# RWKV-7 + MLA + PEER block: the inverse's diagonal blocks through a DRAM tile of their own, four gates' weights in another pool

## The chip, the cores and the metric

One core of a Trainium2 chip runs the whole kernel in one launch. The metric is the device time of one execution in microseconds (us); less is better. The time of a kernel is the median of several executions.

## What is computed

One transformer-like block on T = 512 tokens of width 1024, in float32. The normed input is multiplied by one large matrix `w_in`; its columns are cut into three parts: 15 chunks of 128 columns for an RWKV-7 time mix, 4 for a latent attention (MLA), and 16 for gates. Both mixes run on the same input, each is projected back, multiplied by a sigmoid gate and added; a PEER layer (16,384 experts, top 16 of 8 heads) and a small gated projection follow. Cut to what matters here:

```python
def rwkv7_scan(r, a_vec, b_vec, v, k, decay):
    def step(state, inp):
        r_t, a_t, b_t, v_t, k_t, w_t = inp
        sa = jnp.einsum('bdhvk,bdhk->bdhv', state, a_t)
        state = (state * w_t[..., None, :] + sa[..., :, None] * b_t[..., None, :]
                 + v_t[..., :, None] * k_t[..., None, :])
        return state, jnp.einsum('bdhvk,bdhk->bdhv', state, r_t)
...
def hybrid_rwkv7_mla_peer_block(...):
    u = rmsnorm(x, g_mix) @ w_in
    y_rw = rwkv7_time_mix(u[..., :RW_COLS], ...)
    y_mla = mla_mix(u[..., RW_COLS:RW_COLS + MLA_COLS], ...)
    g = sigmoid(u[..., RW_COLS + MLA_COLS:])
...
```

The scan runs in two directions (d = 0, 1) over 8 heads of width 64. It is not computed token by token: the kernel cuts the 512 tokens into 8 chunks of 64, builds for each chunk, head and direction a 64x64 triangular matrix from products of the vectors, and needs the inverse of that triangle. It inverts the two 32x32 diagonal blocks of each (128 of these pairs: 2 directions, 8 heads, 8 chunks) and gets the rest by matmuls.

## The kernel before

The work around the change has three stages. Everything is written with a tile framework: a tile belongs to a pool with a number of buffers, the framework puts in the semaphores, and a scheduler that simulates the program sets the order of the instructions of each engine. Every engine then executes its own list in that order. A pool that is allocated where a released pool stood waits for the last use of the released pool's tiles.

**Preparation (`prep`, L353 on, driven together with `others` and the first six gates from L641 on).** For each pair of heads c = 0 to 3 and direction d it makes the scan's vectors and calls three helpers. `gram` (L453) forms the products of the vectors on TensorE (PE, L464), masks them on VectorE (DVE) into a tile `gm` (L466, 3 buffers) in two halves of four chunks, and stores each half by two DMAs that POOL issues (L470) into the DRAM tile `pk_d`, the packed operands of the scan. Then SyncE (SP) reads the 32x32 diagonal blocks back from `pk_d` into the tile `U` (L478): 4 DMAs per call, of 8 partitions x 32 rows x 32 numbers, so 32 in all. Last DVE multiplies `bk` by the decay (L480). `bkt_` (L482) transposes `bk` on PE (L488), copies it on ScalarE (ACT, L489) and POOL stores it (L491). `v_t` does the same for `v` (L496 to L505) and makes `bonus` (L508 to L511). After the last of them the pool of this stage, `P`, is released, and the pools of the next stage (`YM`, `M`, `GW`) are allocated.

**The inverse, the gates and the start of attention (L944 on).** `inverse` (L555) does the 128 inversions at once, one pair of blocks per partition: 31 steps, k from 31 down to 1, each a product `xtmp` (L567) and a sum into `X` (L570) for each of the two blocks b = 0, 1, so 124 DVE instructions in sequence. `X` is stored (L574, L575) for the scan's chain. Beside it, gates 6 to 15 are computed. A gate (`gates`, L634) is one chunk of `w_in`: SP loads the raw weights of 512 KB (`wload`, L123; 3 raw buffers `wraw`), ACT rounds them into `whi` (L132), DVE makes the rest `wlo` (L133), PE does 24 matmuls of 128x512 (`mm3`, L137 to L143: for each of the 8 slices one with `whi` and `xh`, one with `whi` and `xl`, one with `wlo` and `xh`), ACT takes the sigmoid (L637), SP stores it (L638). `whi` and `wlo` come from a pool that the caller names or, without a name, from the pool `s.W` (2 buffers, shared with the weights of the attention). The loop at L947 gives gates 6 to 9 no pool; the one at L952 gives gates 10 to 15 the pool `GW`, which has 2 buffers and lies where `P` lay.

```python
inverse()
rest = attn()
for _ in gates(NG, NG + GK, GT):
    pass
...
for _ in gates(NG + GK, 16, GT, GW):
    pass
GW.release()
CH = pool(name="ch", bufs=2)
drive(chain(), rest, ...)
```

NG is 6, GK is 4; GT is the PSUM tag `mm`, whose two buffers the gates share with the first matmuls of the attention: 12 for `vt` (L831), split by ACT and DVE (L147, L148), then the first projections (`proj_k`, `proj_q`; their splits are `kl`, `ql` on L148 and `rt` on L854 to L856) and scores (L874).

**The chain (`chain`, L652).** Its pool `CH` lies where `GW` lay, and its operands `pk` are loaded into the space of `xh` and `xl`, which the gates read. So its first work, two memsets on POOL (L657) and the load of `pk` (L667), waits for the last gate's last matmul. Its steps are then interleaved with the attention.

In the changed kernel the lines from 274 on stand one further down, and those behind the new store in `gram` five further: L638 there is L643, L567 is L572, L464 is L465, L488 is L493. The new store is L473.

Of the kernel before, what the change touches and what calls it, by code (L numbers as in the profile page):

```python
# [20 lines left out]
F32 = mybir.dt.float32  # L21
# [91 lines left out]
def phase1(nc, tc, A, dbg):  # L113

    s = K()
# [65 lines left out]
    def mm_tile(shape=(128, 512), tag="mm"):  # L181
        return (ppc if tag in "cu" else pp).tile(list(shape), F32, name=tag, tag=tag, bufs=1 if tag == "u" else None)
# [76 lines left out]
    def uchunk(oc, tag="mm", pl=None, raw=None):  # L259
        hi, lo = raw or wload(A["w_in"][oc], pl)  # L260
        ps = mm_tile(tag=tag)
        mm3(ps, hi, lo, *(XR if raw else (xh, xl)), [(k, k) for k in range(8)])
        return ps
# [6 lines left out]
    pk_d = gdram.tile([16, 128, 2048], F32, name="pk_d")  # L270
    v_d = gdram.tile([128, 8, 8, 64], F32, name="v_d")
    x_d = gdram.tile([128, 2, 32, 32], F32, name="x_d")
    xt_d = gdram.tile([128, 32, 32], F32, name="xt_d")

    s.WX = pool(name="w0", bufs=1, side="right")
    MU = pool(name="mu", bufs=2)
# [5 lines left out]
    U = R.tile([128, 2, 32, 32], F32, name="U", tag="Oa")  # L282
# [52 lines left out]
    def prep():  # L335
# [117 lines left out]
        def gram(c, d):  # L453

            AR = B["ar", c, d]
            BKf = B["bk", c, d].rearrange("p c a t -> p c (a t)")
            for half in range(2):
                gm = P.tile([128, 4, 2, 2, 64], F32, name="gm", bufs=3)
                for q in range(2):
                    sl = slice(q * 64, q * 64 + 64)  # L460
                    ps = mm_tile((128, 4, 128), tag="c")
                    for i in range(4):
                        cc = half * 4 + i
                        nc.tensor.matmul(ps[:, i], BKf[sl, cc], AR[sl, cc].rearrange("p a t -> p (a t)"),  # L464
                                         start=True, stop=True)  # L465
                    nc.vector.tensor_mul(gm[:, :, q], ps.rearrange("p i (a t) -> p i a t", a=2),  # L466
                                         mask[:, None].to_broadcast([128, 4, 2, 64]))
                gf = gm.rearrange("p c q a t -> p c (q a t)")
                for e, r0, o in ((1, d * 64, c * 256), (0, 64 - d * 64, d * 1024 + c * 256)):
                    (nc.gpsimd, nc.sync)[GQ if e else 0].dma_start(  # L470
                        pk_d[half * 8 + e:half * 8 + 8:2, r0:r0 + 64, o:o + 256].rearrange("k s t -> s k t"),
                        gf[r0:r0 + 64])

            for q in range(2):
                for b in range(2):
                    r0, p0 = d * 64 + b * 32, d * 64 + (2 * c + q) * 8
                    o = (2 * c + q) * 128 + b * 32
                    nc.sync.dma_start(U[p0:p0 + 8, b], pk_d[1::2, r0:r0 + 32, o:o + 32])  # L478

            nc.vector.tensor_mul(BKf, BKf, WC[:, d, c, :, None].to_broadcast([128, 8, 128]))  # L480

# [38 lines left out]
        for c in range(4):  # L520
            u_k(c)
            w_a(c, 0)
            u_r(c)
            k_norm(c)
            abkr(c, 0)
            yield UNS
            w_a(c, 1)
            if c:
                gram(c - 1, 1)
                u_v(c)  # L530
                bkt_(c - 1, 1)
                v_t(c - 1)
            else:
                u_v(c)
            abkr(c, 1)
            if c == 2:
                shifted(14, lg)
                nc.scalar.activation(lg, lg, AF.Sigmoid)
            yield UNS
            if c < 3:  # L540
                gram(c, 0)
                yield 100
                bkt_(c, 0)
        gram(3, 0)
        gram(3, 1)
        yield UNS
# [86 lines left out]
    def gates(i0, i1, tag="u", pl=None):  # L633
        for i in range(i0, i1):  # L634
            ps = uchunk(19 + i, tag, pl)
            gt = MU.tile([128, T], F32, name="gt")
            nc.scalar.activation(gt, ps, AF.Sigmoid)  # L637
            nc.sync.dma_start(gates_d[i], gt)  # L638
            yield UNS
# [9 lines left out]
    GW = pool(name="gw", bufs=2)  # L649
# [294 lines left out]
    inverse()  # L944
    Oa = R.tile([128, 4, T], F32, name="Oa")
    rest = attn()
    for _ in gates(NG, NG + GK, GT):  # L947
        pass
    if PRE:
        while next(rest) >= 0:  # L950
# [93 lines left out]
GT = "mm"  # L1044
# [6 lines left out]
GK = 4  # L1051
NG = 6
# [495 lines left out]
```

## Time and profile before

| what | value |
|---|---|
| median of 3 executions | 1909.32 us (1908.85 to 1920.4) |
| the profiled execution: its own time | 1914.83 us |
| its span, first to last instruction | 1912.7 us |
| outside the span (difference) | 2.1 us |
| mean granted TensorE clock | 0.982 |

The profile is of one execution. Times in its rows count from the span's start. PE is TensorE's matmuls, PEld its weight loads, DVE VectorE, ACT ScalarE, POOL GpSimd, SP SyncE (which here only issues DMAs; SPq is its queue of instructions). A row of a timeline gives start, length, engine, line, operation, output and inputs, how many instructions it joins, and in brackets how long the engine had been idle and for what. Matmuls overlap in their records: one that takes 0.39 us in its row starts 0.23 us after the one before. The stages named above lie at about 187 to 263 us (the end of preparation), 263 to 329 us (inverse and gates) and from 329 us (chain).

### The profile page before, as it was taken

To read this page: it belongs to the slowest core of one execution; us is meant where nothing else is said; L and a number is where in the kernel's file an instruction comes from. 1 tells how busy PE (TensorE), PEld (TensorE's weight loads), DVE (VectorE), ACT (ScalarE), POOL (GpSimd) and SP (SyncE) were. 2 spreads that over 40 slices of the span, in tenths; PEclk is the share of its full clock that TensorE was granted. 3 is DMA by queue.
4 is the path that set the end of the run, shared out by engine and by line. 5 is a ranking of instruction groups with operands and counts; after the bars stand their busy time and mean duration, and the time that the engine had idled before them with its cause. 6 is when DMAs were issued, how large, how long until landed. Compare 5 with 4: busy or idle time off the path is not lost.

```text
span 1912.7 us, 29780 instructions
## 1 busy us (share of the span) xinstructions
PE 1821.6 (95%) x10969; PEld 1569.8 (82%) x10969; DVE 1540.8 (81%) x3103; ACT 827.2 (43%) x1224; POOL 468.4 (24%) x449
## 2 busy tenths in 40 slices
PE   7999869999999998999999999999999999999997
PEld 6777647777677888999999989888888888888775
DVE  6865778889855889999898965878788788778777
ACT  4755533666334333444444433333333333333354
POOL 1012331220101000332233021334344354344100
PEclk9999989999999999999999999999999999999999
DMA  4355664763434333889999899899999999999862
GB/s 166 90 151 174 165 179 144 226 204 105 149 105 143 100 100 100 260 289 347 339 342 327 307 354 350 315 338 340 338 335 343 322 352 340 340 327 335 280 214 99
DMA packets 196721, 470.19 MB, mean 246 GB/s; under 512 B 33312, under 2 KB 100896, under 8 KB 192736
## 3 DMA queue, kind: packets, MB, share of 16 engines
q1 hardware_dynamic: 146688, 273.23, 43.4%
q0 software_dynamic: 49744, 194.80, 28.7%
q8 instruction: 86, 1.41, 0.3%
q14 instruction: 59, 0.48, 0.1%
q10 hardware_dynamic: 144, 0.26, 0.0%
HBM read 397.97 MB, written 70.25 MB: 245 GB/s over the span
## 4 chain that ended last, share of the span: by engine, by line
PE 69%; DVE 13%; DMA 10%; issue 5%; ACT 3%; POOL 0%; SPq 0%; DVEq 0%; POOLq 0%; ACTq 0%
PE po L1498 20%; PE pa L1150 7%; PE pa L1148 7%; PE pa L1149 7%; DMA row<-in_v,e 6%; PE mm L141 3%; PE mm L142 3%; PE mm L143 3%; DVE wlo L133 2%; PE po L1377 2%; PE q L141 2%; PE q L142 2%; PE q L143 2%; DVE acc L1103 1%; DMA gt<-gates_d 1%
## 5 line engine op out<-in xcount | busy, mean ns | idle before, releaser
L132 ACT ACTIVATE whi<-wraw 128x1024 fp32r<-128x1024 f32 x352 | 370.4, 1058 | 429.7 <-PE pa L1149 157.4
L133 DVE TENSOR_TENSOR wlo<-wraw,whi 128x1024 fp32r<-128x1024 f32 x352 | 428.3, 1221 | 89.6 <-ACT whi L132 82.9
L1150 PE MATMUL pa<-hh,wlo 128*128 128x384 f32 x1024 | 348.9, 341 | 4.3 <-DVE wlo L133 4.3
L1148 PE MATMUL pa<-hh,whi 128*128 128x384 f32 x1024 | 348.9, 341 | 3.5 <-ACT gs L1156 2.5
L1149 PE MATMUL pa<-hl,whi 128*128 128x384 f32 x1024 | 348.3, 340 | 0.0
L1085 POOL DMA_INDIRECT row<-in_u,e x128 | 165.6, 1293 | 423.9 <-DVE row L1093 326.9
L1498 PE MATMUL po<-wlo,wh 128*128 128x512 f32 x768 | 239.1, 392 | 4.3 <-DVE wlo L133 4.3
L1085 POOL DMA_INDIRECT row<-in_v,e x128 | 178.5, 1395 | 248.6 <-DVE acc L1103 234.2
L1498 PE MATMUL po<-whi,wl 128*128 128x512 f32 x768 | 238.4, 392 | 0.0
L1498 PE MATMUL po<-whi,wh 128*128 128x512 f32 x768 | 211.0, 390 | 4.5 <-issue 3.4
L1103 DVE SCALAR_TENSOR_TENSOR acc<-row,pre,acc 128x1024 f32<-128x1024 f32 x127 | 162.7, 1281 | 54.8 <-DMA row<-in_v,e 54.2
L1148 PEld LDWEIGHTS pa<-hh,whi 128*128 128x128 f32 x1024 | 193.2, 189 | 8.2 <-ACT gs L1156 3.2
L1150 PEld LDWEIGHTS pa<-hh,wlo 128*128 128x128 f32 x1024 | 193.0, 189 | 6.6 <-DVE wlo L133 4.6
L1149 PEld LDWEIGHTS pa<-hl,whi 128*128 128x128 f32 x1024 | 193.0, 188 | 3.8
L1498 PEld LDWEIGHTS po<-wlo,wh 128*128 128x128 f32 x768 | 144.6, 189 | 32.4 <-DVE wlo L133 5.1
L1498 PEld LDWEIGHTS po<-whi,wl 128*128 128x128 f32 x768 | 145.3, 189 | 30.9
L1093 DVE SCALAR_TENSOR_TENSOR row<-row,h2t 128x1024 f32<-128x1024 f32 x128 | 155.4, 1220 | 17.5 <-DMA row<-in_u,e 17.4
L1498 PEld LDWEIGHTS po<-whi,wh 128*128 128x128 f32 x768 | 143.0, 188 | 29.4 <-issue 3.6
L147 ACT ACTIVATE wh<-gl 128x384 fp32r<-128x384 f32 x72 | 37.9, 526 | 214.3 <-PE po L1498 214.2
L147 ACT ACTIVATE wh<-ga 128x384 fp32r<-128x384 f32 x48 | 25.2, 524 | 128.2 <-PE po L1498 83.2
L141 PE MATMUL mm<-xh,whi 128*128 128x512 f32 x184 | 74.5, 405 | 4.9 <-ACT gt L637 3.3
L1297 ACT ACTIVATE st<-g 128x512 f32<-128x512 f32 x96 | 50.9, 600 | 54.3 <-PE g L1296 54.3
(465 smaller groups left out, 3178.7 us busy)
## 6 DMA issues: line engine op xcount, KB each, us to landing
wraw<-in_uT SPq DMA_DIRECT2D x128, 512.0 KB
wraw<-in_v SPq DMA_DIRECT2D x128, 512.0 KB
gd<-st POOLq DMA_DIRECT2D x12, 2048.0 KB, 8.2
g<-gd SPq DMA_DIRECT2D x32, 768.0 KB
wraw<-in_w_in SPq DMA_DIRECT2D x35, 512.0 KB
pk<-pk_d SPq DMA_DIRECT2D x16, 1024.0 KB
ga_d<-gs SPq DMA_DIRECT2D x72, 192.0 KB
gl<-ga_d SPq DMA_DIRECT2D x72, 192.0 KB
```

Of the source, the lines that this page charges most:

```text
L132: nc.scalar.activation(hi, raw, AF.Copy)
L133: (nc.gpsimd if s.nw <= NWP else nc.vector).tensor_sub(lo, raw, hi.bitcast(F32))
L141: nc.tensor.matmul(out, hi[:, kw], xh[:, kx], start=(i == 0), stop=False)
L142: nc.tensor.matmul(out, hi[:, kw], xl[:, kx], start=False, stop=False)
L143: nc.tensor.matmul(out, lo[:, kw], xh[:, kx], start=False, stop=(i == n - 1))
L1085: nc.gpsimd.indirect_dma_start(out=r, out_offset=None, in_=table, in_offset=bass.IndirectOffsetOnAxis(ap=e3[:, hk:hk + 1], axis=0))
L1093: nc.vector.scalar_tensor_tensor(r, r, 1.0, h2t, op0=OP.mult, op1=OP.mult, accum_out=pre[:, u:u + 1])
L1103: nc.vector.scalar_tensor_tensor(acc, r, pre[:, u:u + 1], acc, op0=OP.mult, op1=OP.add)
L1148: nc.tensor.matmul(pa, hi[:, k], hh[:, k, 0:NDT], start=(k == 0), stop=False)
L1149: nc.tensor.matmul(pa, hi[:, k], hl[:, k, 0:NDT], start=False, stop=False)
L1150: nc.tensor.matmul(pa, lo[:, k], hh[:, k, 0:NDT], start=False, stop=(k == 7))
L1498: nc.tensor.matmul(po[tb][:, half], w[:, ts], v[:, hs], start=(m == 0 and w is wh and v is vh), stop=(m == 127 and w is wl))
```

## The change

There are two edits. First, `gram` stores the diagonal blocks a second time: for each half, block b and head of the pair q, SP issues one DMA from `gm` into a new DRAM tile `u_d` (32 rows, 4 chunks, 32 numbers), so 8 per call and 64 in all. The reads of `U` come from `u_d` and no more from `pk_d`; there are 2 per call, 16 in all, and each moves 16 rows of 1024 numbers in one piece. Second, gates 6 to 9 are given the pool `GW`.

```diff
+    u_d = gdram.tile([8, 2, 2, 8, 32, 32], F32, name="u_d")
...
+                for b in range(2):
+                    r0 = d * 64 + b * 32
+                    for q in range(2):
+                        nc.sync.dma_start(u_d[d * 4 + c, b, q, half * 4:half * 4 + 4].rearrange("k s t -> s k t"),
+                                          gm[r0:r0 + 32, :, q, 0, b * 32:b * 32 + 32])
                 gf = gm.rearrange("p c q a t -> p c (q a t)")
...
-            for q in range(2):
-                for b in range(2):
-                    r0, p0 = d * 64 + b * 32, d * 64 + (2 * c + q) * 8
-                    o = (2 * c + q) * 128 + b * 32
-                    nc.sync.dma_start(U[p0:p0 + 8, b], pk_d[1::2, r0:r0 + 32, o:o + 32])
+            p0 = d * 64 + c * 16
+            for b in range(2):
+                nc.sync.dma_start(U[p0:p0 + 16, b], u_d[d * 4 + c, b].rearrange("q k s t -> (q k) s t"))
...
-    for _ in gates(NG, NG + GK, GT):
+    for _ in gates(NG, NG + GK, GT, GW):
         pass
```

The scheduler then makes other lists. On PE, before, two gates stand among the last small matmuls of preparation (the first rows of gate 6, behind the products L464 of the pair c = 2; ident is the identity of a transpose):

```order
L488 MATMUL c<-ident,bk 128x128 x8
L503 MATMUL c<-ident,vRS 128x128 x8
L510 MATMUL c<-sht,same 128x512
L464 MATMUL c<-ar,bk 128x128 x16
L141 MATMUL mm<-xh,whi 128x512
L142 MATMUL mm<-xl,whi 128x512
L143 MATMUL mm<-xh,wlo 128x512
```

The same place on PE after the change, up to the first matmul of gate 6:

```order
L227 MATMUL c<-ident,spr 128x128 x4
L415 MATMUL c<-lw,w_242 128x512
L419 MATMUL c<-la,a_244 128x512
L465 MATMUL c<-ar,bk 128x128 x16
L493 MATMUL c<-ident,bk 128x128 x8
L508 MATMUL c<-ident,vRS 128x128 x8
L515 MATMUL c<-sht,same 128x512
L465 MATMUL c<-ar,bk 128x128 x32
L493 MATMUL c<-ident,bk 128x128 x16
L508 MATMUL c<-ident,vRS 128x128 x8
L515 MATMUL c<-sht,same 128x512
L141 MATMUL mm<-xh,whi 128x512
```

The 48 matmuls of gates 6 and 7 have left preparation: all ten gates now stand behind its last matmul, in the order 6, 7, 8, 9, the 12 matmuls of `vt`, the first projections, and 10 to 15. The four `whi` on ACT and the four `wlo` on DVE that belong to gates 6 to 9 have left preparation with them.

On DVE, before, the first `wlo` beside the inverse (that of the attention's weights) stands here, at the steps of 135 and 156 numbers (X_2056 and X_2057 are the two blocks):

```order
L570 TENSOR_TENSOR X_2056<-X_2056,xtmp 128x27x5
L570 TENSOR_TENSOR X_2057<-X_2057,xtmp 128x27x5
L133 TENSOR_TENSOR wlo<-wraw,whi 128x1024
L567 TENSOR_TENSOR xtmp<-U,X_2056 128x156
L567 TENSOR_TENSOR xtmp<-U,X_2057 128x156
```

After the change the first `wlo` on DVE beside the inverse are those of gates 6 and 7:

```order
L572 TENSOR_TENSOR xtmp<-U,X_2105 128x192
L572 TENSOR_TENSOR xtmp<-U,X_2106 128x175
L133 TENSOR_TENSOR wlo<-wraw,whi 128x1024
L575 TENSOR_TENSOR X_2105<-X_2105,xtmp 128x24x8
L575 TENSOR_TENSOR X_2106<-X_2106,xtmp 128x25x7
L133 TENSOR_TENSOR wlo<-wraw,whi 128x1024
L148 TENSOR_TENSOR cql<-cqn,cqh 128x512
```

The `wlo` of gate 6 stands behind 28 instructions of the inverse and one for `bonus`; the two blocks now run one step apart. Further down DVE's list, before, the two `kl` splits, which free the PSUM buffer that gate 10 takes, stand among the growing steps:

```order
L567 TENSOR_TENSOR xtmp<-U,X_2056 128x252
L567 TENSOR_TENSOR xtmp<-U,X_2057 128x252
L148 TENSOR_TENSOR kl_2373<-mm,kh_2370 64x512
L570 TENSOR_TENSOR X_2056<-X_2056,xtmp 128x18x14
L570 TENSOR_TENSOR X_2057<-X_2057,xtmp 128x18x14
L567 TENSOR_TENSOR xtmp<-U,X_2056 128x255
L148 TENSOR_TENSOR kl_2374<-mm,kh_2371 64x512
```

After the change they stand here on DVE:

```order
L148 TENSOR_TENSOR kl_2422<-mm,kh_2419 64x512
L572 TENSOR_TENSOR xtmp<-U,X_2105 128x207
L572 TENSOR_TENSOR xtmp<-U,X_2106 128x220
L575 TENSOR_TENSOR X_2105<-X_2105,xtmp 128x9x23
L575 TENSOR_TENSOR X_2106<-X_2106,xtmp 128x10x22
L148 TENSOR_TENSOR kl_2423<-mm,kh_2420 64x512
```

The second `kl` has 90 of the inverse's 124 instructions ahead of it, and 8 `wlo`; before it had 57 and 4. SP's list at the end of preparation, after the change, is nine stores to `u_d`, a read of `U`, a store, a read, six stores, two reads; the raw weights of gates 6 to 8 are loaded before these, that of gate 9 behind them.

## Rows read from the trace of the kernel before

**Rows 1.** Stretches: length, busy (instructions) by engine, PEclk granted, DMA share, GB/s.
```profile
210.00:228.00 18.00, 16.58 (x75) 11.82 (x74) 10.01 (x18) 12.10 (x14) 3.40 (x5) 1.00 0.54 184
228.00:259.20 31.20, 21.04 (x144) 16.44 (x143) 23.05 (x35) 13.10 (x20) 16.43 (x23) 0.89 0.84 226
259.20:272.70 13.50, 13.42 (x49) 10.18 (x49) 9.20 (x21) 4.65 (x8) 5.56 (x6) 0.87 0.29 91
272.70:293.60 20.90, 8.75 (x20) 5.00 (x21) 20.18 (x51) 6.54 (x10) 0.00 (x0) 0.67 0.44 126
293.60:329.20 35.60, 35.58 (x153) 28.66 (x154) 29.01 (x84) 11.60 (x15) 0.00 (x0) 1.00 0.41 141
329.20:480.00 150.80, 137.80 (x2182) 111.91 (x2181) 134.06 (x291) 98.09 (x191) 28.02 (x51) 0.94 0.59 180
```

**Rows 2.** POOL's timeline: beside the inverse's start, and the chain's first work.
```profile
265.52 3.80 POOL L840 TENSOR_TENSOR kl<-krt,kh 32x512 fp32r<-32x512 f32 x3
329.68 1.06 POOL L657 MEMSET Xs<- 128x512 f32 x2 [60.37 <-PE mm L143]
```

**Rows 3.** PE's waits, 240 to 345 us: waiting line, releaser, us, times, longest.
```profile
PE mm L831 <- DVE wlo L133: 6.4, 1, 6.4
...
PE mm L831 <- DVE vt L148: 2.9, 1, 2.9
...
PE mm L141 <- DVE kl L148: 1.6, 1, 1.6
```

**Rows 4.** DVE's timeline: end of preparation, start of the inverse, `kl`, late step.
```profile
211.94 1.21 DVE L480 TENSOR_TENSOR bk<-bk,wc 128x1024 f32<-128x1024 f32 x1
...
227.00 1.22 DVE L133 TENSOR_TENSOR wlo<-wraw,whi 128x1024 fp32r<-128x1024 f32 x1
228.13 0.68 DVE L402 TENSOR_TENSOR kk<-kk,c 128x512 f32<-128x512 f32 x1
...
250.12 1.28 DVE L466 TENSOR_TENSOR gm<-c,mask 128x512 f32<-128x512 f32 x2
...
263.35 0.50 DVE L567 TENSOR_TENSOR xtmp<-U,X 128x31 f32<-128x31 f32 x2 [6.71 <-DMA U<-pk_d]
...
265.54 2.61 DVE L570 TENSOR_TENSOR X<-X,xtmp 128x60 f32<-128x60 f32 x2
...
292.79 0.69 DVE L148 TENSOR_TENSOR kl<-mm,kh 64x512 fp32r<-64x512 f32 x1
...
320.78 0.35 DVE L570 TENSOR_TENSOR X<-X,xtmp 128x60 f32<-128x60 f32 x2
```

**Rows 5.** ACT's timeline: first work in the space of preparation's pool.
```profile
263.42 1.68 ACT L147 ACTIVATE cqh<-cqn 128x512 fp32r<-128x512 f32 x3 [4.22 <-DMA pk_d<-bkt]
```

**Rows 6.** PE's timeline: gate 6 and the transposes behind it, the last gate matmul.
```profile
210.11 0.50 PE L141 MATMUL mm<-xh,whi 128*128 128x512 f32 x1
...
215.79 1.03 PE L488 MATMUL c<-ident,bk 128*128 128x128 f32 x8
...
329.17 0.40 PE L143 MATMUL mm<-xh,wlo 128*128 128x512 f32 x1
```

**Rows 7.** Issue of the reads of `U`: ns min/median/max, first and last start.
```profile
L478 SPq DMA_DIRECT2D U<-pk_d x32: 264/365/1242, 107.0 to 259.3; - x32
```

**Rows 8.** The stores L470 by POOL: from issue to landing.
```profile
DMA to landing us min/median/max: 3.1/4.1/6.0
```

**Rows 9.** The chain of waits, 200 to 420 us: start, length, what.
```profile
259.26 4.26 DMA U<-pk_d
```

**Rows 10.** DMA, 200 to 262 us: SP's queue: packets, MB, share of 16 engines.
```profile
q1 hardware_dynamic: 5487, 2.26, 14.2%
```

**Rows 11.** DVE by line, 263.3 to 321.5 us: busy us, mean ns, idle before.
```profile
L570 DVE TENSOR_TENSOR X<-X,xtmp 128x31 f32<-128x31 f32 (+15 forms) x62 | 21.3, 377 | 0.0
L567 DVE TENSOR_TENSOR xtmp<-U,X 128x31 f32<-128x31 f32 (+15 forms) x62 | 20.8, 367 | 6.9 <-DMA U<-pk_d 6.7
L133 DVE TENSOR_TENSOR wlo<-wraw,whi 128x1024 fp32r<-128x1024 f32 x8 | 9.8, 1219 | 0.5 <-ACT whi L132 0.4
```

## The prediction

> **What bounds the kernel now.** I read the stretches around the change first, then the first work of the stage that follows it, then PE's waits, and last the timelines of DVE, ACT and PE. A change here counts by what it does to the start of the chain: from 329.2 to 480 us PE is busy for 137.80 of 150.80 us and DVE for 134.06 [rows 1], so a stage that starts later has little slack to catch up with. What releases the chain is plain: its first memset on POOL had been waiting for 60.37 us and starts 0.1 us after the last gate matmul [rows 2, 6]. The inverse does not release it: its last steps run at 320.78 [rows 4], over 8 us earlier.
>
> So the question is when the tenth gate ends. The reader sees two very different stretches ahead of it. From 293.6 on PE is full (35.58 of 35.6 us) with 153 matmuls: six gates of 24 and 9 of scores, 0.2325 us each, 5.6 us for a gate. From 272.7 to 293.6 it is busy for only 8.75 of 20.9 us, at a granted clock of 0.67, while DVE is busy for 20.18 [rows 1]. The waits name DVE each time: 6.4 us for a `wlo`, 2.9 us for a `vt` split, 1.6 us for the `kl` split that frees gate 10's PSUM buffer [rows 3]. DVE is the bound of this stage, by its order: inverse and splits share one list. Gates 6 to 9 hardly feel it in the kernel before, because gates 6 and 7 are computed during preparation and the weights of 8 and 9 are split there.
>
> **The end of preparation.** The second edit takes two gates, four `whi` and four `wlo` out of it. Gate 6 holds PE from 210.11 to 215.79, and the transposes L488 come right behind; their input `bk` was ready at 211.94 + 1.21 = 213.15 [rows 4, 6], so they can start 2.6 us earlier. The `wlo` at 227.00 keeps `kk` until 228.13: another 1.1 us [rows 4]. Together 3.8 us. Bounds: 1.1 us if only the last of these lies on the path; 7.8 if the other gate's and splits' time does too (gate 7's 5.6 us and the 2.2 us of two more `wlo`). I take 3.8, the sum of the two that I can point at. Then the last `gm`, done at 250.12 + 1.28 = 251.40 [rows 4], comes at 247.6, and the last store of `bkt`, for which the first ACT work in the old pool's space waits until 263.42 [rows 5], lands at 259.6. That store matters more than it did: gates 6 and 7 now take `GW`, in that space, so no `whi` for them can be written before.
>
> **The short way to U.** Before, 263.35 - 251.40 = 11.95 us pass from the last `gm` to the first step of the inverse [rows 4]. After, they are four stores of 0.365 us to issue, 1.5 us [rows 7]; a landing; two reads to issue, 0.7 us; a landing. No row shows a store of 16 KB or a read of 16 rows of 4 KB. POOL's stores of 256 KB land after 3.1 to 6.0 us, 4.1 in the median [rows 8]; the old read took 4.26 in the chain [rows 9]. Two landings are thus 6.2 at the least and 12 at the most by these rows, the whole way 8.4 to 14.2. I take 9.0, near the low end, because both transfers move less than those timed. The inverse starts at 256.6, 6.8 us earlier. Bounds, with those of preparation: 252.0 and 264.5.
>
> Each piece of the new stores is 128 bytes, 64 times 128 pieces in all. SP's queue, whose pieces in this stretch were nearly all of that size, took 14.2% of 16 engines over 62 us, 141 us of engine time for 5487 packets, 26 ns each [rows 10]; 512 pieces of the last half call, spread over 16 engines, are 0.8 us. Inside the bounds. The Trainium skill (DMA: Bandwidth & Descriptors, Specifications) speaks against the edit: under 512 bytes a transfer falls short of line rate, since the engine reads and writes back. No row here prices a store of that size; were it to double the packet's 26 ns, the 0.8 us would be 1.6 and the forecast 0.8 us later. The same page (Anatomy of one DMA) gives about 2.0 us plus bytes over 436e3 for a DMA that POOL issues, by which both landings together would be an estimated 4.2 us, the inverse would start about 2.6 us earlier than in my sum and the forecast would be 1916; the 3.1 us that the fastest of 32 stores took here [rows 8] says no.
>
> **Gates beside the inverse.** This is where the gain goes. In DVE's new list the `wlo` of gate 6 has 28 steps of the inverse ahead of it and the second `kl` has 90, with 8 `wlo`; before they were 57 and 4. One step costs 0.34 us: the lines L567 and L570 have 42.1 us busy for 124 instructions [rows 11] (their records, 377 and 367 ns in the mean, overlap a little). A `wlo` costs 1.13, as the one at 227.00 does before `kk` [rows 4]. From the inverse's start to the end of the second `kl` there were 30.1 us [rows 4]; now 33 more steps, 11.2 us, 4 more `wlo`, 4.5 us, and the `bonus` instruction, 0.6 us: 46.4 us. Bounds: 42.6 if POOL's `kl`, 3.80 us from 265.52 on, no longer meets the inverse (the pair of 60 numbers took 2.61 us beside it, and 0.35 later on [rows 2, 4]), 49 if DVE waits for weights twice. I take 46.4, since POOL's `kl` follows the same store as before and still falls into the inverse.
>
> So `kl` is done at 256.6 + 46.4 = 303.0, and gate 10 starts there. Behind it stand the same six gates and 8 or 9 matmuls of scores, 35.6 us [rows 1]: the last gate ends at 338.6 instead of 329.17 + 0.4, 9 us later. PE by itself would be sooner: gate 6 cannot finish before its `wlo`, about 256.6 + 28 x 0.34 + 0.6 + 1.1 = 267.8; from there 92 matmuls of gates 6 to 9, 12 of `vt` and 9 of projections (26.3 us), 1.8 us for a clock that is low after the pause (13.5 us at 0.87 granted where gate 8 starts [rows 1]), and 35.6: 331.5, 1.9 us later than before. The later one decides; some 7 us of PE's pause in front of gate 10 stay.
>
> The sum: 9 us on the profiled 1914.83 us. Its span of 1912.7 and the 2.1 us around it are 5.5 us over the median of the executions shown, so on the median the forecast is 1909.3 + 9 = 1918 us. The inverse itself, with all 12 `wlo` in its list, ends about where it did, and nobody waits for that.
>
> **Rivals.** *The short way reaches the chain (faster).* Gates need no split in time, PE runs without pause from the first `whi`. It can start at 259.6 + 1.06, and ten gates, `vt`, projections and scores are 240 + 12 + 9 + 9 matmuls, 62.8 us, with 1.8 for the clock: 325.3, 4.3 us sooner, 1905 us. For it: preparation does become shorter, and PE's total work is unchanged. Against it: DVE must have the `wlo` of gate 6 by 261 and the second `kl` 35.6 us before the end. It decides if the inverse starts before about 247, where the last `gm` is only just made; or if DVE's list matters less than its records say.
>
> *No change to speak of.* PE's bound above holds instead of DVE's: +1.9 us, 1911 us. For it: PE idles 12 of 20.9 us before [rows 1], room for the moved gates. It needs DVE to lose the 3.8 us of POOL's `kl` and the inverse to start 3.3 us sooner than I say.
>
> *SP becomes the bound (slower still).* SP works strictly in order: each read of `U` waits for stores to land, and behind it wait the next stores, whose `gm` (3 buffers) cannot be written again until they land. In the last two calls a store, a read, a store and a read stand singly in the list. Two more waits of one landing, 4.1 us each [rows 8], delay the last `gm` and with it all that follows: +17 us, 1926 us. For it: the reads of `U` came last before the inverse already [rows 4]. Against it: with three buffers two halves are in flight.
>
> **How the numbers follow.** The forecast, +4 to +14 us, gets 0.5; no change, -2 to +4, 0.22; the faster rival, -2 to -8, 0.13; SP's, over +14, 0.15. A measurement of this kernel tells about 1% from no change, 19 us. Only the tails pass it: SP's rival with a third wait, 0.05 slower; a faster rival of four times its price, 0.03. Leaving one in ten on each side gives 1904 to 1930 us; the forecast's own range is 1913 to 1923.
>
> **What would show it.** Right: first step of the inverse at 255 to 259 us; preparation's last PE work about 4 us sooner; first gate matmul at about 260, then a pause of several us for `wlo`; PE idle again before gate 10 with DVE named; POOL's first memset of the chain at 335 to 341 us. Wrong: that memset before 329.7; or an inverse that starts no earlier, with SP's queue waiting for stores to `u_d`; or a full PE between 268 and 300 us, which would mean that DVE was not the bound.

## The result and the profile after

The changed kernel takes 1938.83 us (median of 4 executions, 1935.74 to 1939.6); the kernel before, beside it, 1909.87. The ratio of the times is 1.0129, 95% interval 1.0104 to 1.0154, which is 25 us slower; the two medians differ by 29. The forecast was 1918, the range ended at 1930. The sign and the place were right and the size was not.

The profiled execution has a span of 1937.4 us, 24.7 more than before. The first memset of the chain on POOL shows that 21.2 of them are there already (329.68 before [rows 2]):

```profile
350.88 1.07 POOL L662 MEMSET Xs<- 128x512 f32 x2 [76.96 <-PE mm L143]
```

The other 3.5 us are behind it. In the ten profiles below in which the whole computation is done, the span behind this memset is between 1576 and 1591 us (1583.0 before, 1586.5 after), with and without the stores, so these 3.5 us can't be told from nothing, and the runs below are compared by their moments up to the memset first.

DVE's timeline of the changed kernel shows the same moments as [rows 4], with the first `wlo` (that of gate 6):

```profile
225.00 0.69 DVE L403 TENSOR_TENSOR kk<-kk,c 128x512 f32<-128x512 f32 x1 [1.27 <-PE c L227]
...
243.70 2.63 DVE L467 TENSOR_TENSOR gm<-c,mask 128x512 f32<-128x512 f32 x4 [0.39 <-PE c L465]
...
253.57 1.29 DVE L467 TENSOR_TENSOR gm<-c,mask 128x512 f32<-128x512 f32 x2 [3.03 <-DMA u_d<-gm]
267.27 0.20 DVE L572 TENSOR_TENSOR xtmp<-U,X 128x31 f32<-128x31 f32 x1 [12.41 <-DMA u_d<-gm]
...
278.05 1.23 DVE L133 TENSOR_TENSOR wlo<-wraw,whi 128x1024 fp32r<-128x1024 f32 x1 [0.21 <-issue]
...
314.25 0.69 DVE L148 TENSOR_TENSOR kl<-mm,kh 64x512 fp32r<-64x512 f32 x1
```

`kk` is 3.1 us earlier than before. The four `gm` behind it are not; before they started at 243.37:

```profile
243.37 2.63 DVE L466 TENSOR_TENSOR gm<-c,mask 128x512 f32<-128x512 f32 x4 [0.17 <-PE c L464]
```

Nor is the last `gm`: it ends at 254.86 instead of 251.40, after a wait for the new stores. The inverse starts at 267.27 instead of 263.35. The second `kl` ends at 314.94, 47.7 us later.

PE's timeline, with the rows that answer to [rows 6]:

```profile
211.78 1.94 PE L493 MATMUL c<-ident,bk 128*128 128x128 f32 x8 [3.12 <-DVE bk L485]
...
269.58 0.80 PE L141 MATMUL mm<-xh,whi 128*128 128x512 f32 x1 [7.83 <-ACT whi L132]
...
279.33 0.79 PE L143 MATMUL mm<-xh,wlo 128*128 128x512 f32 x1 [7.58 <-DVE wlo L133]
...
315.08 0.47 PE L141 MATMUL mm<-xh,whi 128*128 128x512 f32 x1 [1.81 <-DVE kl L148]
```

The transposes behind the pair c = 2 do start 4 us earlier (215.79 before), but take 1.94 us where they took 1.03 [rows 6]: PE had been idle for 3.12 us, and runs at the lower of its two clock levels (1.2 instead of 2.4 GHz). The stretches (columns as in [rows 1]) say it for all of the end of preparation, where the granted clock was 1.00 up to 228 us and 0.89 from there to 259 [rows 1]:

```profile
210.00:228.00 18.00, 11.57 (x36) 7.75 (x37) 9.27 (x18) 11.34 (x14) 3.72 (x6) 0.53 0.42 102
228.00:247.00 19.00, 14.78 (x96) 12.86 (x96) 15.94 (x24) 6.61 (x10) 9.25 (x14) 0.64 0.71 178
247.00:262.00 15.00, 8.95 (x39) 5.79 (x38) 4.17 (x6) 3.37 (x6) 5.52 (x9) 0.67 0.83 213
262.00:290.00 28.00, 12.84 (x43) 9.56 (x44) 20.84 (x50) 7.46 (x9) 5.98 (x7) 0.63 0.32 84
```

And from the first matmul that waited for gate 6's `wlo` to the last gate's end, PE is busy for 66.35 of 71.6 us:

```profile
279.30:350.90 71.60, 66.35 (x267) 51.65 (x268) 51.21 (x128) 25.29 (x34) 0.02 (x1) 0.95 0.44 143
```

### The profile page after: what moved, and what is told of

The parts are those of the page before. It is cut to its first block, busy times and chain, and to the rows that moved or that the text cites. A ratio compares the mean times of both kernels' runs of the same rounds, so it can differ in the third digit from the quotient of the medians.

```text
span 1937.4 us, 29874 instructions
## 1 busy us (share of the span) xinstructions
PE 1829.4 (94%) x10969; PEld 1574.6 (81%) x10969; DVE 1542.5 (80%) x3103; ACT 826.4 (43%) x1224; POOL 465.6 (24%) x449
## 4 chain that ended last, share of the span: by engine, by line
PE 79%; DVE 11%; DMA 3%; ACT 3%; issue 2%; SPq 0%; POOL 0%; DVEq 0%; ACTq 0%; POOLq 0%
PE po L1503 27%; PE pa L1153 8%; PE pa L1155 8%; PE pa L1154 8%; PE mm L141 3%; PE mm L142 3%; PE mm L143 3%; DVE wlo L133 2%; PE po L1382 2%; PE q L141 2%; PE q L142 2%; PE q L143 2%; PE g L1300 1%; PE g L1301 1%; PE c L465 1%
## 5 line engine op out<-in xcount | busy, mean ns | idle before, releaser
L1098 DVE SCALAR_TENSOR_TENSOR row<-row,h2t 128x1024 f32<-128x1024 f32 x128 | 155.4, 1221 | 12.4 <-DMA row<-in_u,e 12.3
L143 PE MATMUL mm<-xh,wlo 128*128 128x512 f32 x184 | 73.8, 402 | 7.6 <-DVE wlo L133 7.6
L142 PE MATMUL mm<-xl,whi 128*128 128x512 f32 x184 | 74.0, 402 | 0.0
```

Of the source, the lines that this page charges most:

```text
L142: nc.tensor.matmul(out, hi[:, kw], xl[:, kx], start=False, stop=False)
L143: nc.tensor.matmul(out, lo[:, kw], xh[:, kx], start=False, stop=(i == n - 1))
L1098: nc.vector.scalar_tensor_tensor(r, r, 1.0, h2t, op0=OP.mult, op1=OP.mult, accum_out=pre[:, u:u + 1])
```

## Experiments

Twelve kernels were run. For each the moments are from its own profile and the ratio is that of the times; "last gm" is the end of the last `gm`, "kl" the end of the second `kl`, "memset" the start of the chain's first.

| kernel | last gm | inverse starts | kl | memset | ratio [95% interval] |
|---|---|---|---|---|---|
| before | 251.4 | 263.4 | 293.5 | 329.7 | 1 |
| changed | 254.9 | 267.3 | 314.9 | 350.9 | 1.0129 [1.0104, 1.0154] |
| e1 stores alone | 253.2 | 266.6 | 299.4 | 336.0 | 1.0068 [1.0043, 1.0092] |
| e2 pool alone | 251.0 | 260.4 | 306.6 | 342.6 | 1.0096 [1.0068, 1.0123] |
| e4 filler matmuls | 254.5 | 264.1 | 311.4 | 347.4 | 1.0095 [1.0066, 1.0123] |
| e8 gates 6, 7 back | 252.1 | 264.0 | 301.7 | 337.7 | 1.0075 [1.0050, 1.0101] |
| e9 one read | 253.5 | 263.5 | 312.2 | 348.1 | 1.0110 [1.0053, 1.0167] |
| e10 stores unread | 255.3 | 268.1 | 314.1 | 351.5 | 1.0141 [1.0088, 1.0194] |
| e11 half the inverse | 255.3 | 265.0 | 309.1 | 344.6 | 1.0159 [1.0088, 1.0230] |
| e12 POOL's wlo | 251.1 | 260.4 | 294.9 | 331.0 | 1.0025 [1.0000, 1.0050] |
| e13 raw weights apart | 255.3 | 267.4 | 316.2 | 352.6 | 1.0146 [1.0120, 1.0172] |
| e14 both of these | 255.7 | 267.9 | 311.3 | 346.8 | one time, 1941.33 us |
| e15 three buffers | 254.3 | 266.6 | 313.0 | 349.5 | one time, 1942.15 us |
| e16 before, raw apart | 250.4 | 262.2 | 291.7 | 327.9 | 1.0001 [0.9984, 1.0018] |

**The two edits apart.** e1 keeps the stores and reads of `u_d` and takes the pool away from gates 6 to 9; e2 is the kernel before with the pool alone.

```diff
-    for _ in gates(NG, NG + GK, GT, GW):
+    for _ in gates(NG, NG + GK, GT):
```

> The blocks go through u_d, but gates 6 to 9 keep their old pool, so the scheduler puts gates 6 and 7 back into the end of preparation. Theory A (both edits cost, the second more): the stores hold gm and SP, the last gm comes about 3 us later than in the kernel before and the inverse starts at about 266 us instead of 263.4; all behind it is shifted by 3 to 4 us: about 1913 us, chain's first memset at about 333 us. Theory B (the stores through SP are the whole loss): the inverse starts at 267 us or later and the kernel takes 1930 us or more. Theory C (the short way works and only the moved gates cost): the inverse starts at 257 to 260 us and the time is 1905 us.

> Gates 6 to 9 take GW, U is read from pk_d as before. Theory A: the clock is at its lower level in much of 210 to 262 us (0.55 to 0.7 granted in the mean), so the end of preparation gains nothing; the inverse starts at 262 to 264 us, 46 to 48 us later the second kl is done, 36 us later the last gate ends: chain's first memset at about 346 us, 1927 us in all. Theory B: no loss without the stores, 1905 to 1912 us, memset at 330 us. Theory C: most of the loss, 1935 us or more.

e1: 1924.93 us, e2: 1928.29 us, beside 1910.54. Each edit alone makes the kernel slower, by 0.7% and 1.0%; together 1.3%, not quite their sum. The first lies between A (1913 us) and B (1930 or more); its inverse starts at 266.6 us as A said, its memset 3 us later than A's. The second came within 2 us of theory A's time, its `kl` 46.2 us after the inverse's start, and B's and C's numbers for it both fall. Its inverse starts 1.6 us before A's range and 3.0 us sooner than in the kernel before, though its last `gm` is only 0.4 us sooner. DVE's timeline of e2, read the old way from `pk_d`, shows that the old way is no longer than the new one:

```profile
249.75 1.29 DVE L466 TENSOR_TENSOR gm<-c,mask 128x512 f32<-128x512 f32 x2 [2.59 <-DMA pk_d<-gm]
...
260.37 0.30 DVE L567 TENSOR_TENSOR xtmp<-U,X 128x31 f32<-128x31 f32 x2
...
266.33 1.62 DVE L133 TENSOR_TENSOR wlo<-wraw,whi 128x1024 fp32r<-128x1024 f32 x1
```

From the last `gm` to the inverse it takes 9.3 us here and in e12, 11.8 in e16 and 12.0 in the kernel before; the way through `u_d` takes 9.6 to 13.3 in nine profiles, 12.4 in the changed kernel. Each kernel has one profile, and the old way alone spreads over 2.7 us, so a difference of that size in the start of the inverse proves nothing by itself.

**The clock in the end of preparation.** e4 adds 48 matmuls whose results nobody reads, where the kernel before had gates 6 and 7.

```diff
+        def warm(n):
+            pw = mm_tile(tag="mm")
+            for i in range(n):
+                nc.tensor.matmul(pw, xh[:, i % 8, 0:128], xh[:, (i + 1) % 8], start=(i == 0), stop=(i == n - 1))
...
                 v_t(c - 1)
+                if c == 3:
+                    warm(24)
+                    warm(24)
```

> The changed kernel with 48 more matmuls of 128x512 on xh, whose results nobody reads, in the end of preparation, where the kernel before had gates 6 and 7. Theory A1 (the low clock costs the end of preparation about 3 us): granted clock 0.9 or more from 210 to 228 us, but the 48 matmuls take PE's time as the gates did; the last gm is at 253 to 255 us and the inverse starts at 264 to 268 us: within 4 us of the changed kernel, 1935 to 1940 us. Theory A2 (the low clock is the main loss): the inverse starts 6 us or more sooner, 1930 us or less.

1928.86 us. From 210 to 228 us the granted clock is now 1.00. The stretch, then DVE's timeline:

```profile
210.00:228.00 18.00, 16.72 (x85) 12.19 (x84) 8.27 (x16) 11.83 (x15) 3.20 (x5) 1.00 0.35 94
```

```profile
225.19 0.69 DVE L403 TENSOR_TENSOR kk<-kk,c 128x512 f32<-128x512 f32 x1 [0.81 <-PE c L227]
...
240.42 2.62 DVE L467 TENSOR_TENSOR gm<-c,mask 128x512 f32<-128x512 f32 x4
...
253.18 1.29 DVE L467 TENSOR_TENSOR gm<-c,mask 128x512 f32<-128x512 f32 x2 [5.94 <-DMA u_d<-gm]
```

The four `gm` start 3.3 us sooner than in the changed kernel, with 48 matmuls more and `kk` at the same time. Single moments shift between kernels (e9, below, has its four `gm` at 240.54 without any filler, because its `kk` comes at 222.37), so the distance counts. From `kk` to the four `gm` it is 15.0 to 15.7 us in the six profiles whose clock from 210 to 228 us is 1.00, this one among them, and 18.0 to 19.6 us in the eight where it is 0.50 to 0.62. So the lower clock costs about 3 us there, as A1 had it.

It does not reach the last `gm`, which is only 0.4 us sooner: the wait for the stores grows from 3.0 to 5.9 us and takes the gain. The inverse is 3.2 us sooner, not the 6 that A2 wanted, and the memset 3.5 us; but 2.8 of these lie between the last `gm` and the inverse (9.6 us instead of 12.4), and e11 has 9.7 there at the low clock. That they come from the clock is not shown. The time gained 0.3% by the ratios and came out at A2's number; the intervals of the two ratios overlap.

**Gates 6 and 7 back.** e8 leaves `GW` to gates 8 and 9.

```diff
-    for _ in gates(NG, NG + GK, GT, GW):
+    for _ in gates(NG, NG + 2, GT):
+        pass
+    for _ in gates(NG + 2, NG + GK, GT, GW):
```

> As the changed kernel, but gates 6 and 7 have no pool of their own again (gates 8 and 9 keep GW), and stand in the end of preparation as before. Theory A (what the moved gates cost is the two gates that must now run behind the inverse's start, and the wlo in DVE's list): 48 matmuls leave the stage beside the inverse, the second kl has about 80 steps ahead of it: chain's first memset at 335 to 340 us, 1918 to 1924 us. Theory B (stores): no change against the changed kernel, 1935 us or more. Theory C (any gate in GW costs the same): 1930 us or more, too.

1924.5 us, memset at 337.7: theory A (its time is missed by 0.5 us). Of the 21 us at the memset 13 are gone: 9.9 between the inverse's start and the memset, where the two gates no longer run, and 3.3 by an inverse that starts sooner.

**The stores and the reads.** e9 reads `U` in two DMAs behind the last store, with `u_d` laid out by block first; e10 makes the stores and reads `U` from `pk_d` as before.

```diff
-            p0 = d * 64 + c * 16
-            for b in range(2):
-                nc.sync.dma_start(U[p0:p0 + 16, b], u_d[d * 4 + c, b].rearrange("q k s t -> (q k) s t"))
...
         gram(3, 1)
+        for b in range(2):
+            nc.sync.dma_start(U[:, b], u_d[b].rearrange("e q k s t -> (e q k) s t"))
```

> The changed kernel, but U is read by two DMAs of 512 KB behind the last store (u_d laid out with the block first), so no read stands between two stores on SP. Theory A (reads that wait for stores to land hold up the next stores on SP, and so gm): the wait of gm for u_d's stores (3.0 us in the changed kernel) falls under 1 us, the last gm is done at 251 to 252 us instead of 254.9; the two reads land 4 to 6 us after the last store: inverse starts at 262 to 265 us, 3 us sooner, about 1935 us. Theory B (the stores' own landing of 1.4 to 7.1 us and SP's issue are the whole cost): gm waits as long as before, inverse at 267 us or later, 1938 us.

> Both edits' stores and pools, but U is read from pk_d as before the change: the 64 stores to u_d are made and nobody reads them. Against the run with the pool alone (inverse at 260.4 us, 1928 us) this shows what the stores cost, and against the changed kernel what the new reads give. Theory A (stores cost, new reads give nothing): last gm 2 to 4 us later than 251.0, inverse at 264 to 267 us, 1935 to 1940 us. Theory B (the new reads cost): inverse at 261 us, 1928 us. Theory C (the new reads save 3 us that the stores take): inverse at 269 us or later, 1941 us or more.

e9: 1936.95 us beside 1915.08. Its DVE rows:

```profile
252.16 1.29 DVE L467 TENSOR_TENSOR gm<-c,mask 128x512 f32<-128x512 f32 x2 [4.79 <-DMA u_d<-gm]
263.45 0.20 DVE L570 TENSOR_TENSOR xtmp<-U,X 128x31 f32<-128x31 f32 x1 [3.79 <-DMA U<-u_d]
```

No read stands between stores, and `gm` waits 4.8 us all the same. So for `gm` theory A's reason falls: not the reads in SP's queue hold it, but the stores' own time. For the last stores it holds, as SP's queue shows. In the changed kernel, at the end of preparation (a row gives start, length and number; the last eight stores are those of the last call, and its last half's four start at 260.27):

```profile
244.42 12.28 SPq L473 DMA_DIRECT2D u_d<-gm  x9
257.95 0.31 SPq L483 DMA_DIRECT2D U<-u_d  x1
258.32 0.48 SPq L473 DMA_DIRECT2D u_d<-gm  x1
258.91 0.37 SPq L483 DMA_DIRECT2D U<-u_d  x1
259.33 3.66 SPq L473 DMA_DIRECT2D u_d<-gm  x6
264.60 2.12 SPq L483 DMA_DIRECT2D U<-u_d  x2
```

```profile
260.27 2.72 SPq L473 DMA_DIRECT2D u_d<-gm  x4
```

In e9:

```profile
254.44 2.73 SPq L473 DMA_DIRECT2D u_d<-gm  x4
258.62 0.84 SPq L548 DMA_DIRECT2D U<-u_d  x2
```

The last four stores could go when the last `gm` was done, at 254.86; SP gets to them 5.4 us later. In e9 it is 1.0 us, and 3.7 to 5.4 in all nine kernels with reads among the stores. Two things fill the queue: two reads with their waits (256.70 to 259.33, some 2 us besides a store), and the issue itself, which takes up to 1.76 us for a store here, 12.28 us from the first to the last of the nine. The last sixteen stores of the changed kernel:

```profile
L473 SPq DMA_DIRECT2D u_d<-gm x16: 316/1016/1760, 244.4 to 261.7; - x16
```

Why issuing is slow there is not shown. e9's inverse starts at 263.5, in A's range; its two large reads take longer (4.8 us from issue to the first step, 2.7 in the changed kernel), so its whole way, 10.0 us, is no shorter than e4's or e11's.

e10: 1942.55 us, `gm` waits 4.7 us, inverse at 268.1 (its second block's first step at 273.0), memset at 351.5, 8.9 us later than in e2, which differs by the stores alone. So the stores cost about 9 us by these two profiles; the ratios differ by 0.45%, with intervals that overlap. B falls; the time is in C's range, the inverse between A's and C's. The new reads give 0.6 us back at the memset, and 0.1% by the ratios, within their intervals.

The 64 DMAs `u_d<-gm` (L473) of the changed kernel, 16 KB each, from the start of issue to landing:

```profile
DMA to landing us min/median/max: 1.4/3.3/7.1
```

The 16 reads of `U` (L483) behind them, 64 KB each:

```profile
DMA to landing us min/median/max: 2.0/3.1/5.0
```

**What bounds the stage beside the inverse.** e11 leaves out the steps of the inverse's second block (62 DVE instructions). e13 puts the raw weights of gates 8 to 15 into `GW`; e14 does both; e15 gives `GW` three buffers.

```diff
-            for b in range(2):
+            for b in range(1):
                 nc.vector.tensor_mul(t[b], ...
...
-            for b in range(2):
+            for b in range(1):
                 nc.vector.tensor_add(X[b][:, 0:k, k:], ...
```

> The changed kernel with the steps of the inverse's second block left out: 62 DVE instructions fewer, PE and the gates' weights the same. Theory A (DVE's list bounds the stage): 60 steps instead of 90 ahead of the second kl, about 10 us less: kl done 37 to 39 us after the inverse's start instead of 47.7, chain's first memset at 339 to 343 us instead of 350.9. Theory B (the gates' weights or PE bound it): memset within 3 us of 350.9.

The second `kl` comes 44.2 us after the inverse's start, not 37 to 39, and the memset at 344.6, 6.3 us sooner, of which 2.3 are an earlier start. (What lies behind works on other values here, so the whole time isn't compared.) DVE has room now and waits for weights, in PE's, ACT's and DVE's waits from 260 to 350 us:

```profile
DVE wlo L133 <- ACT whi L132: 17.2, 6, 4.4
ACT whi L132 <- PE mm L142: 13.4, 6, 4.1
ACT whi L132 <- DMA wraw<-in_wkv: 11.3, 1, 11.3
```

Neither theory holds alone. In the changed kernel ACT waits 13.5 us for the raw weights of the attention, which could be loaded only when gate 7's `wlo` had freed a raw buffer:

```profile
268.47 2.00 ACT L132 ACTIVATE whi<-wraw 128x1024 fp32r<-128x1024 f32 x2 [7.87 <-DVE xtmp L572]
...
285.57 2.01 ACT L132 ACTIVATE whi<-wraw 128x1024 fp32r<-128x1024 f32 x2 [13.53 <-DMA wraw<-in_wkv]
```

So that was tried.

```diff
-        raw = (pl if own else s.W).tile([128, 8, 128], F32, name="wraw", ...)
+        if apart:
+            raw = pl.tile([128, 8, 128], F32, name="wraw", bufs=2)
+        else:
+            raw = (pl if own else s.W).tile([128, 8, 128], F32, name="wraw", ...)
...
-    GW = pool(name="gw", bufs=2)
+    GW = pool(name="gw", bufs=3)
```

> The changed kernel with the raw weights of gates 8 to 15 in GW too (2 buffers more), so the attention's two weights can be loaded during preparation instead of waiting for the wlo of gates 6 and 7 to free a raw buffer. In the run with half of the inverse left out DVE waited 17 us for whi and the second kl came only 3.5 us sooner. Theory W (the weights' way wlo, raw buffer, load of 4.6 us, whi bounds the stage as much as DVE): ACT's wait of 13.5 us for the attention's weights is gone, the second kl comes 41 to 45 us after the inverse's start instead of 47.7, memset at 344 to 348 us. Theory D (DVE's list alone; it now has about 100 steps but 6 wlo ahead of the kl): 47 to 48 us, memset within 2 us of 350.9.

> Both at once: raw weights apart and the second block of the inverse left out. Theory W (two bounds of about one length, DVE's list and the weights' way): only now does the stage become much shorter: second kl 34 to 39 us after the inverse's start (44.2 with half the inverse alone), memset 7 us or more sooner than in that run's 344.6, counted from the inverse's start. If the bound is a third thing (PE, or the scores): 43 us or more.

> The changed kernel with three buffers in GW instead of two, so the whi of gate 8 need not wait for gate 6's last matmul. Theory W with the weights' own buffers as its cause: second kl 41 to 44 us after the inverse's start. With the raw buffers as its cause, or theory D: 46 us or more.

e13, 1940.47 us: the wait for the load is gone and nothing is gained; `kl` 48.7 us after the inverse's start, memset at 352.6: near theory D's 47 to 48, with 99 steps ahead of `kl` instead of 90. But ACT idles 13.9 us at the same place, by the profile until a DVE step of the inverse, so the run removed one cause of that pause and not the pause. e15: 46.3 us, memset at 349.5, 0.7 us sooner when counted from the inverse's start; the weights' own buffers aren't it either. e14: 43.4 us and a memset 78.9 us after the inverse's start (79.6 in e11): W falls. What it shows instead is PE (its lines stand three further down; up to gate 10 no wait of 0.7 us or more is left out behind the first row):

```profile
278.87 0.80 PE L146 MATMUL mm<-xh,wlo 128*128 128x512 f32 x1 [6.55 <-DVE wlo L136]
...
303.32 0.50 PE L839 MATMUL mm<-whi,cqh 128*128 128x512 f32 x1 [0.70 <-ACT gt L645]
...
311.40 0.47 PE L144 MATMUL mm<-xh,whi 128*128 128x512 f32 x1 [1.65 <-DVE kl L151]
```

From gate 6's `wlo` on PE is almost without a pause, and the stage ends 67.8 us later (68.7 in e11); in the changed kernel it is 71.6, with 5.3 us of pauses. So with half the inverse PE's own work (64.3 us of the 67.8) is most of what is left, and gate 6's `wlo` is what it starts from. Half the steps bring that `wlo` little: it comes 9.7 us after the inverse's start instead of 10.8, for POOL's three `kl` run beside the inverse's first steps, three of which take 1.2 us each in e14. That an earlier `wlo` alone would help is not shown: in e2 it comes 6.0 us after the inverse's start, and the memset 82.2 us after it, against 83.6 in the changed kernel.

**Two tries at a better version.** e12 and e16 start from the kernel before: POOL makes the `wlo` of gates 8 to 11; the raw weights of gates 10 to 15 lie in `GW`.

```diff
-        (nc.gpsimd if s.nw <= NWP else nc.vector).tensor_sub(lo, raw, hi.bitcast(F32))
+        (eng or nc.vector).tensor_sub(lo, raw, hi.bitcast(F32))
```

> The kernel before the change, with the wlo of gates 8 to 11 made by POOL instead of DVE. If DVE's list bounds the stage before the change too: PE's pause of 12 us ahead of gate 10 shrinks by 2 to 5 us, memset at 325 to 328 us, about 1907 us. If POOL's wlo holds DVE up as its kl does, or takes more than 4 us: memset at 330 us or later, 1910 us or more.

> The kernel before the change with the raw weights of gates 10 to 15 in GW, a try at a version that beats both: its ACT waited 9.7 us for the raw weights of gates 10 and 11, and PE idled 12 us there. If the weights' way bounds that stage before the change too: memset 3 to 6 us sooner than 329.7, 1905 us, ratio 0.997 or less. If DVE's list does: ratio within 0.2% of 1.

e12, 1920.18 beside 1915.08 us: beside the inverse POOL needs 2.7 and 3.4 us for two `wlo` that DVE makes in 1.2, and the memset is at 331.0 though the inverse had started 3 us sooner, as the second expectation had it. The ratio's interval reaches 1.0000. e16, 1912.39 beside 1912.22: no difference, as for DVE's list. Neither beats the kernel before.

## Why the prediction was wrong

**Right: the stage beside the inverse.** From the inverse's start to the second `kl` 46.4 us were forecast, 47.7 came (46.2 in e2). From there to the last gate 35.6 were forecast, 35.9 came. Counted from gate 6's `wlo` (done at 267.8 by the forecast, 279.3 measured), 70.8 us were forecast and 71.6 came. The pause ahead of gate 10 is there, with DVE named: 1.8 us, and 5.3 in all where some 7 were forecast. So moving two gates behind preparation costs what it was said to cost; e8 gives most of it back.

The length was right; DVE as its one bound was not all of it. A full PE between 268 and 300 us was to show that DVE is not the bound, and PE is full for gates 6 to 9:

```profile
279.30:303.30 24.00, 23.97 (x95) 18.93 (x95) 21.78 (x51) 8.91 (x10) 0.00 (x0) 0.93 0.57 180
```

The forecast had PE 7 us below DVE; e11 and e14 show that with less on DVE only 4 to 5 us are won, counted from the inverse's start, so the two lie closer together than was said.

**Wrong: when the inverse starts.** The step that failed is the start at 256.6 us; it was 267.3, and the 10.7 us of difference went through the stage one for one. With it fell three of the signs that were named: preparation's last PE work was to be 4 us sooner and ends 5.9 us later (261.8 instead of 255.9), the first gate matmul came at 269.58 instead of about 260, the memset at 350.88 instead of 335 to 341. The sign of being wrong came as written, an inverse that starts no earlier, with SP's queue waiting for stores to `u_d` (240 to 268 us):

```profile
SPq L483 <- DMA u_d<-gm: 7.1, 5, 2.2
```

The terms of the 10.7 us:

The end of preparation, 7.3 us. "Together 3.8 us" was the gain of taking gates 6 and 7 out. At `kk` 3.1 us of it were there, and at the four `gm`, which start at 243.70 instead of 243.37, nothing. The term left out is the clock: the gates were what kept PE at its higher clock there (1.00 granted, 0.53 without them), and from `kk` to the four `gm` it takes 3.5 us longer; e4 gives 3.3 of them back. The other term left out is the last `gm`'s wait for the new stores, 3.0 us; between 1.3 and 5.9 in the profiles with the stores, 0 to 2.6, for another store, in those without. The last `gm` was expected at 247.6 and ended at 254.9. The two terms overlap: with the clock back (e4) the wait grows and the last `gm` is 0.4 us sooner; without the stores but at the low clock (e2) it ends at 251.0, no sooner to speak of than before.

The short way, 3.4 us. 9.0 us were taken; it was 12.4. The term put at nothing is SP's queue: 5.4 us pass before the first of the last four stores is issued, behind reads that wait for landings and stores that take 1.0 us each to issue in the median of the last sixteen, where 0.365 was taken from the reads ([rows 7] had 1.24 as its longest). What was in the sum came out shorter than forecast: 4.3 us from there to the first read and 2.7 from that read to the inverse, 7.0 together. So the guess "near the low end, because both transfers move less than those timed" was not the fault.

The price of the small pieces was off too, and did no harm. The 26 ns per packet [rows 10] are the mean of packets of 128 bytes and of 4 KB. From 240 to 260 us in the kernel before, SP's queue moved almost nothing but 128-byte pieces:

```profile
q1 hardware_dynamic: 2379, 0.30, 9.4%
```

9.4% of 16 engines in 20 us are 12.6 ns per packet. In the changed kernel from 200 to 262 us the 128-byte packets of that queue took 13.5 ns in the mean, so the 512 pieces of the last half cost about 0.4 us and not 0.8.

The fixed 2.0 us of the Trainium skill (DMA: Bandwidth & Descriptors, Anatomy of one DMA), given for DMAs that POOL issues, would make an estimated 2.6 us for POOL's stores of 256 KB. This case's trace has 3.1 to 6.0 for them [rows 8], with the DMA engines busy for 0.54 to 0.84 of the time from 210 to 259 us [rows 1]; SP's stores, which that fit is not for, took 3.3 in the median. The warning of the Trainium skill (DMA: Bandwidth & Descriptors, Specifications) that pieces under 512 bytes fall short of line rate doesn't separate the two ways here, since the old reads and the new stores both have them.

**The rivals.** The one that went slower through SP had 0.15 and named most of what happened: `gm` held by stores that have not landed, and reads in SP's queue that hold the next stores. e9 shows that the reads are not what holds `gm`; they hold the last four stores. It was priced by two waits of 4.1 us on `gm`, and one of 3.0 is seen at the end; the slow issue and the clock were in no sum, so that its +17 us came nearer than the forecast's +9 is in part luck. That the faster rival and "no change" needed an inverse at 247 or at 253 us rules both out.

What stays open: why e1, whose inverse starts only 3.2 us late and whose memset is 6.3 us late, is 13 us slower by its ratio (its profiled execution, the slowest of its eight, lost 7.5 us behind the memset, within the spread named above); and why SP needs over 1 us to issue a store at the end of preparation. That `gm` would wait less with a fourth buffer, or the last stores in a queue other than SP's, wasn't tried.

## What to carry to other kernels

Before work is moved out of a stretch to shorten it, ask what keeps TensorE's clock up there: two gates that filled its pauses paid for part of themselves, and behind the stretch they had to be done at full price. A copy made for a shorter way also holds the buffer that it is made from until it has landed. Many small DMAs on one queue have to be issued one after the other, and a read among them that waits for a landing holds all that stand behind it: count the queue's time, and not only the transfers. Where two resources bound a stage within a few us of each other, taking work from one of them shows the other.

## What was not expected of the hardware

The 16 KB stores by SP landed after 1.4 to 7.1 us, 3.3 in the median, against 3.1 to 6.0 for POOL's of 256 KB [rows 8]: a sixteenth of the bytes bought 0.8 us in the median. SP took 0.30 us to issue such a store at the least and up to 1.76 at the end of preparation (up to 2.38 in e4). And 48 matmuls fewer from 210 to 226 us brought PE's granted clock from 1.00 to 0.53 between 210 and 228 us, which made eight transposes take 1.94 us instead of 1.03.
